# Where weight buffers and streamed operands begin, modulo 256 bytes, in a decoder block on one core

## The chip, the core and the metric

One core of a Trainium2 chip runs the whole block. The metric is the time of one execution in device microseconds; a kernel's time is the median of its runs. All arithmetic on data is float32, and TensorE takes it in the format float32r: each factor is cut into a high part that the format holds exactly and a low part, and a product is made of three (high × high, high × low, low × high).

## The reference

A decoder block with 512 positions and 1024 channels: a mixer of a short gated convolution (A) and sparse attention (B), merged by gates, and a feed-forward part of width 2816 with a short convolution.

```
h = rmsnorm(x, norm1_g);  proj = h @ w_in          # 512 x 1024 by 1024 x 4888
y_a = a_b * causal_dwconv(a_c * a_x, conv_a_w)
y_b = nsa(q, compressed k/v, selected k/v, window k/v, gates)    # 8 heads of 64, 2 groups
mix = gm[:D] * (y_a @ w_a_out) + gm[D:] * (y_b @ w_b_out)
x = x + mix @ w_o
h = rmsnorm(x, norm2_g);  gu = h @ w_ffn_in        # 1024 x 5632
g = causal_dwconv(gu[:, :2816], ffn_conv_w) + ffn_conv_b
x = x + (silu(g) * gu[:, 2816:]) @ w_ffn_out
```

## The kernel before

Activations lie with channels on the partitions and the 512 positions along them. A weight tile of 128 output channels (128 × 1024 float32, 512 KB) comes by one DMA into a raw buffer (`wr`, three of them). ScalarE copies it to the high part (`wh`), and VectorE, GpSimd or a DMA that accumulates on a negated copy makes the low part (`wl`). There are two buffers for each of `wh` and `wl`. `dense` then issues the products: a 128 × 128 block of weights is loaded into TensorE, and 512 columns of the activation's high or low part stream past it (256 in the feed-forward part). Each matmul has a weight load of its own. With `lo_last`, the products of the low weights follow those of the high ones; otherwise they alternate.

The stages, in order of time:

- token projection (`pj`, to 65 us): here the activations `xg_h`, `xg_l` are what is loaded, and the weights stream past them, 348 or 350 columns at a time;
- the convolution's channels (`conv_tile`, `pa`), gates (`gate_tile`, `pg`) and the merge of A (`pma`), with attention's products between them; the streamed operands are `xg_h`, `xg_l` and `ya_h`, `ya_l`;
- the merge of B (`pmb`, past `yb_h`, `yb_l`) and the output projection (`po` from `mix_h`, `mix_l`), eight tiles of 16 + 8 products;
- from 377 us, the feed-forward part: pairs of channel tiles as a two-level product (`ff_pair`) with seven block products of 12 matmuls each. `x_forms` makes seven combinations of the input (`xf_h`, `xf_l`). The weight blocks 11 and 12 come from `wh`, `wl` (or, for some, a low part from the buffers `dl`), the block 22 and the sums of blocks from `th`, `tl`, `sh`, `sl` on the right side of the memory. Quarters of the down projection (`pdn`, past `ah`, `al`) lie between the pairs; the rest follows at the end.

Tile pools are stacks of memory, from the left (`sb`, `pa`, `px`, `pf` and others) and from the right (`pw`, `pb`, `pc` and others). In a pool, tiles follow each other in the order of their first use, each rounded up to 32 bytes. Tiles of one tag share its buffers, and a new tile takes the buffer that comes free first in the scheduler's own simulation, which also orders the instructions of every engine. A raw, `wh` or `wl` buffer is `TOKC` = 1048 words wide, 4192 bytes, or 96 more than a multiple of 256. So two neighbouring buffers begin 96 bytes apart modulo 256.

Where tiles of before begin, modulo 256 (weights left, streamed operands right; the distance is the difference, weight minus streamed):

| weights | begin | streamed | begin |
|---|---|---|---|
| `wh`, first and second buffer | 160, 0 | `xg_h`, `xg_l` | 192 |
| `wl`, first and second buffer | 224, 64 | `ya_h`, `ya_l` | 192, 0 |
| `dl` (low parts made by DMA) | 224 | `yb_h`, `yb_l` | 64, 128 |
| `sh`, `sl`, `th`, `tl` | 224 | `mix_h`, `mix_l`, `ah`, `al` | 224 |
| | | `xf_h`, `xf_l` | 192 |

Blocks within a tile lie 512 bytes apart, and streamed rows 1024 or 2048, so that a tile's place modulo 256 is that of all its blocks.

Of the kernel before, what the change touches and what calls it, by code (L numbers as in the profile page):

```python
# [11 lines left out]
F32 = mybir.dt.float32  # L12
F32R = mybir.dt.float32r
# [5 lines left out]
P = 128  # L19
D = 1024  # L20
S = 512
# [19 lines left out]
C_V = C_Q + 256  # L41
C_G = C_V + 256
TOKC = C_G + 24
NW4 = 5
NWR = 3
NE = 3
# [24 lines left out]
INV_FREQ = (10000.0 ** (-np.arange(HALF) / HALF)).astype(np.float32)  # L71
CH = ((0, 350), (350, 700), (700, TOKC))

# [18 lines left out]
def tile_block(ctx: ExitStack, tc: tile.TileContext, xT, pos, par, par2, w_tok, w_a3, w_gate, w_ao, w_bo, w_o,  # L92
               w_ff, w_dn, c_w1, out):
    nc = tc.nc
    sb = ctx.enter_context(tc.tile_pool(name="sb", bufs=1, side="left"))
    ps = ctx.enter_context(tc.tile_pool(name="ps", bufs=1, space=bass.MemoryType.PSUM))
    in_ctx = ExitStack()
    pa = in_ctx.enter_context(tc.tile_pool(name="pa", bufs=1, side="left"))
# [4 lines left out]

    def const(shape, name, dt=F32, pool=sb):
        return pool.tile(shape, dt, name=name, tag=name)

    def w_tmp(name, shape):

        t = pp.tile([P, TOKC], F32, name=name, tag="w4", bufs=NW4)
        v = t[:, :math.prod(shape)]  # L110
        if len(shape) == 2:
            v = v.rearrange("p (a b) -> p a b", a=shape[0])
        elif len(shape) == 3:
            v = v.rearrange("p (a b c) -> p a b c", a=shape[0], b=shape[1])
        return v
# [4 lines left out]
    def d_bank(name):  # L120
        return bank("d", name, 2)
# [28 lines left out]
    def load_w(src, n, name, first=0, mid=False, pool=False, by_dma=False, lo=None, made=False, mixed=False, after=(), hi=None, cuts=(), pieces=False, then=None):  # L150


        raw = sb.tile([P, TOKC], F32, name=f"wr_{name}", tag="wr", bufs=NWR)
        if hi is None:
            hi = sb.tile([P, TOKC], F32R, name=f"wh_{name}", tag="wh", bufs=2)
        if lo is None:
            lo = sb.tile([P, TOKC], F32R, name=f"wl_{name}", tag="wl", bufs=2)
        if mixed:
            to = raw[:, :n].rearrange("p (k a d) -> p k a d", a=2, d=HD)
            for i in range(2):  # L160
                nc.sync.dma_start(to[:, :, i], src[:, i])
        for a, b in ((0, first), (first, n)) if first else ((0, n),):
            at = [a] + [c for c in cuts if a < c < b] + [b]
            if not mixed:
                for c, d in zip(at, at[1:]) if pieces else ((a, b),):
                    by = nc.scalar if c < 2 * first and not mid else nc.sync
                    loads.append(by.dma_start(raw[:, c:d], src[:, c:d]))
            if then is not None and b == first:
                then()
            for a, b in zip(at, at[1:]):  # L170
                splits.append(nc.scalar.activation(hi[:, a:b], raw[:, a:b], AF.Copy))
                if after:
                    behind(splits[-1], after[0])
                if not made:
                    if by_dma:

                        nc.scalar.activation(lo[:, a:b], raw[:, a:b], AF.Copy, scale=-1.0)
                        nc.gpsimd.dma_start(lo[:, a:b], src[:, a:b], accum_op=ALU.add)
                    else:
                        e = nc.gpsimd if pool else nc.vector  # L180
                        m = e.tensor_sub(lo[:, a:b], raw[:, a:b], hi[:, a:b].bitcast(F32))
                        if after:
                            behind(m, after[1])
                        elif len(x_lows) == 1:
                            behind(m, x_lows[0])
        return hi, lo
# [2 lines left out]
    ones_r = const([P, P], "ones", F32R)  # L189
    ones = ones_r.bitcast(F32)  # L190
    nc.gpsimd.memset(ones, 1.0)
    warm = const([P, 1], "warm")
    wu = d_bank("wu")
    for i in range(NWU):
        nc.tensor.matmul(wu[:, 0:P], ones, ones, start=True, stop=True)
# [12 lines left out]
        return [t_bank(f"pj_t{tt}{i}") for i in range(2)] + [o_bank(f"pj_o{tt}")]  # L208


    def y_tile(name):
        return pa.tile([P, 2, TOKC], F32R, name=name, tag="y", bufs=4)

    tok_lo = [y_tile(f"tok_lo{i}") for i in range(4)]

    def tok_products(tt, bank, k, wh, wl, first, last, sums=False):
        ts_ = slice(tt * P, (tt + 1) * P)
# [102 lines left out]
    def behind(later, earlier):  # L320

        tc.add_manual_dep(later.ins, earlier.ins.name,
                          mybir.DependencyInfo(mybir.DependencyClass.NoSync, mybir.DependencyReason.DATA),
                          reason="order")
# [86 lines left out]
            nc.vector.tensor_tensor(tsin[:, i, :, 0:HALF], ns, ghi, op=ALU.mult)  # L411
            nc.vector.tensor_tensor(tsin[:, i, :, HALF:], sn, glo, op=ALU.mult)

    mhalf = const([P, 12], "mhalf")
    nc.gpsimd.memset(mhalf, -0.5)

    def rsqrt(dst, src, n):
# [40 lines left out]

    def kv_products(i):
        raw = pp.tile([P, 4 * P], F32, name=f"wr_kv{i}", tag="wrkv", bufs=2)  # L460
        hl = sb.tile([P, TOKC], F32R, name=f"wl_kv{i}", tag="wl", bufs=2)
        n = 4 * P
        d = nc.sync.dma_start(raw.rearrange("p (a c) -> p a c", a=2),
                              w_a3[0:2, :, 2 * P * i:2 * P * (i + 1)].rearrange("a p c -> p a c"))
        behind(d, loads[-1])
        loads.append(d)
        nc.scalar.activation(hl[:, 0:n], raw, AF.Copy)
        nc.vector.tensor_sub(hl[:, n:2 * n], raw, hl[:, 0:n].bitcast(F32))

        def products():  # L470
            for kv in range(2):
                if i == 0:
                    kv_acc.append(d_bank(f"pkc{kv}"))
                units = [(hl[:, c:c + P], hl[:, n + c:n + c + P], xg_h[:, 2 * i + k, :], xg_l[:, 2 * i + k, :])
                         for k, c in enumerate((2 * kv * P, (2 * kv + 1) * P))]
                dense(kv_acc[kv], units, first=i == 0, last=i == 3)
        return products

    def between(k):
        if k in kv_made:  # L480
            kv_made.pop(k)()
        if k == KD - 2:
            t = pp.tile([P, TOKC], F32R, name="sq_hl", tag="w4", bufs=NW4)
            sq_hl.extend((t[:, 0:S], t[:, S:2 * S]))
# [32 lines left out]
    r1b, _ = as_rows("n1", r1, scales1[2])  # L517
# [176 lines left out]
                    nc.vector.tensor_sub(kl4[own, :, g, ks], pv[own], kg[own].bitcast(F32))  # L694


    yb_h = y_tile("yb_h").rearrange("p a c -> p (a c)")[:, 0:4 * S].rearrange("p (a s) -> p a s", a=4)
    yb_l = y_tile("yb_l").rearrange("p a c -> p (a c)")[:, 0:4 * S].rearrange("p (a s) -> p a s", a=4)

    ends = {}  # L700

# [113 lines left out]
        nc.gpsimd.tensor_sub(yb_l[dst], yo, yb_h[dst].bitcast(F32))  # L815


    ya_h = y_tile("ya_h").rearrange("p a c -> p (a c)")[:, 0:4 * S].rearrange("p (a s) -> p a s", a=4)
    ya_l = y_tile("ya_l").rearrange("p a c -> p (a c)")[:, 0:4 * S].rearrange("p (a s) -> p a s", a=4)

    def causal_conv(dst, u, w, bias=None):

# [113 lines left out]
        return raw  # L936

    def form_a1(f, n, raw, form):
        h = sb.tile([P, TOKC], F32R, name=f"wh_s{n}_{f}", tag="wh", bufs=2)
        if (f, n) in A1_BY_DMA:  # L940
            l = lo_by_dma(f"s{n}_{f}", raw, w_ff[f, n])
            nc.scalar.activation(h[:, 0:D], raw[:, 0:D], AF.Copy)
        else:
            l = sb.tile([P, TOKC], F32R, name=f"wl_s{n}_{f}", tag="wl", bufs=2)
            ends["a1"] = split(h[:, 0:D], l[:, 0:D], raw[:, 0:D])
        form["a11"] = (h[:, 0:half], l[:, 0:half])
        form["a12"] = (h[:, half:D], l[:, half:D])
# [91 lines left out]
    px = ctx.enter_context(tc.tile_pool(name="px", bufs=1, side="left"))  # L1039
    x1 = const([P, KD, S], "x1", F32, px)  # L1040

    xf_h = const([P, 4, 7, TH], "xf_h", F32R, px)
    xf_l = const([P, 4, 7, TH], "xf_l", F32R, px)
    xv_ctx = ExitStack()
# [39 lines left out]
    _, sums2, r2b, rows2 = row_scales(sq2, "n2", d_bank)  # L1084
# [4 lines left out]
    pf = ctx.enter_context(tc.tile_pool(name="pf", bufs=1, side="left"))  # L1089
    u_bufs = []  # L1090
    for i in range(NU):
        u = const([P, 2, S + 2], f"c{i}", F32, pf)
        nc.gpsimd.memset(u[:, :, 0:2], 0.0)
        u_bufs.append(u)
    a_hl = {}

    def pair_tile(name, tag):
# [72 lines left out]
    def down_weights(f0, n, j0, by_dma=False):  # L1170

        nm = f"d{f0}{j0}"
        per = D // (n * P)
        raw = sb.tile([P, TOKC], F32, name=f"wr_{nm}", tag="wr", bufs=NWR)
        h = sb.tile([P, TOKC], F32R, name=f"wh_{nm}", tag="wh", bufs=2)
        block = lambda t: t[:, 0:D].rearrange("p (j c) -> p j c", j=per)
        src = w_dn[j0:j0 + per, :, f0 * P:(f0 + n) * P].rearrange("j p c -> p j c")
        nc.sync.dma_start(block(raw), src)
        if by_dma:

            l = lo_by_dma(nm, raw, src, block, after={(0, per): ends["sh"], (0, 2 * per): ends["a1"]}.get((f0, j0)))
            m = nc.scalar.activation(h[:, 0:D], raw[:, 0:D], AF.Copy)
            if (f0, j0) == (0, per):
                behind(m, ends["sh"])
        else:
            l = sb.tile([P, TOKC], F32R, name=f"wl_{nm}", tag="wl", bufs=2)
            split(h[:, 0:D], l[:, 0:D], raw[:, 0:D])
        return h, l

# [102 lines left out]
```

## Time and profile before

| what | value |
|---|---|
| median of three runs | 724.03 us (723.95 to 724.71) |
| the profiled execution | 725.49 us, of which the span from first to last instruction is 723.6 |
| TensorE | busy 716.9 us, 4275 matmuls (an fp32 one counts twice) |
| TensorE's weight loads | busy 637.1 us |
| VectorE, ScalarE, GpSimd | 575.6, 415.3, 125.4 us |
| the chain that ended last | 92% TensorE |
| granted clock of TensorE | 1.0 |
| DMA | 88.19 MB, 122 GB/s on average |

How to read it: a row of the timeline or of a group has the line of the kernel, the engine, the operation and the tiles as out<-in, for a matmul out<-streamed,weights. Timeline rows give start and duration in us, and neighbouring instructions of one kind are merged into one row with their count. Group rows give the busy time in us and the mean duration in ns of one instruction. A matmul's duration overlaps with the next matmul's, so the sum of durations is longer than the time.

### The profile page before, as it was taken

The page shows a single profiled execution, that of the slowest core. Times are in us where ns is not written, and L with a number is a line of the kernel's source. Part 1 is how long each engine was busy: PE and PEld are TensorE (multiplying, and loading weights), DVE is VectorE, ACT ScalarE, POOL GpSimd, SP SyncE. Part 2 cuts the span into 40 slices and gives each one's busy share as a digit, 9 for nine tenths or more (in the row PEclk, how much of TensorE's full clock was granted, in tenths as well). Part 3 has the DMA queues.
Part 4 walks back from the last instruction along what each step waited for, and adds up shares of the span by engine and source line. Part 5 has one row for each costly group of instructions (what it writes and reads, how often), then busy time and mean ns, then how long its engine had stood idle before and what let it go on. Part 6 is the DMA issues. An engine that isn't in the chain of part 4 may idle for free.

```text
span 723.6 us, 11196 instructions
## 1 busy us (share of the span) xinstructions
PE 716.9 (99%) x4275; PEld 637.1 (88%) x4275; DVE 575.6 (80%) x988; ACT 415.3 (57%) x706; POOL 125.4 (17%) x111
## 2 busy tenths in 40 slices
PE   8999999999999999999999999999999999999997
PEld 8999788888888888878889999999999999999986
DVE  7978967587666675887876998998898988989833
ACT  7776555777767767544665665565445554455320
POOL 1122443343343201231002011010000010000000
PEclk9999999999999999999999999999999999999999
DMA  8633552211111211336446476545655556552413
GB/s 292 227 89 115 145 119 79 60 68 58 59 59 59 87 60 59 116 124 210 160 131 161 117 175 152 169 119 131 164 143 127 136 127 154 128 146 88 117 30 116
DMA packets 36804, 88.19 MB, mean 122 GB/s; under 512 B 7440, under 2 KB 10896, under 8 KB 36752
## 3 DMA queue, kind: packets, MB, share of 16 engines
q1 hardware_dynamic: 30672, 74.42, 32.3%
q0 software_dynamic: 5648, 12.58, 10.7%
q8 instruction: 33, 0.54, 0.3%
q10 hardware_dynamic: 432, 0.49, 0.2%
q14 instruction: 19, 0.16, 0.1%
HBM read 85.39 MB, written 2.10 MB: 121 GB/s over the span
## 4 chain that ended last, share of the span: by engine, by line
PE 92%; issue 4%; DMA 2%; POOL 0%; ACT 0%; DVE 0%; SPq 0%; POOLq 0%; DVEq 0%
PE p L147 8%; PE p L143 8%; PE p L140 8%; PE pdn L143 4%; PE pdn L140 4%; PE pg L145 4%; PE pg L140 4%; PE pg L143 4%; PE pdn L147 4%; PE pa L140 3%; PE pa L143 3%; PE pt L792 2%; PE po L143 2%; PE po L140 2%; PE po L147 2%
## 5 line engine op out<-in xcount | busy, mean ns | idle before, releaser
L140 PE MATMUL p<-xf_h,sh 128*128 128x256 f32 x352 | 87.3, 281 | 0.0
L143 PE MATMUL p<-xf_l,sh 128*128 128x256 f32 x352 | 87.2, 281 | 0.0
L140 PEld LDWEIGHTS p<-xf_h,sh 128*128 128x128 f32 x352 | 66.3, 188 | 0.0
L143 PEld LDWEIGHTS p<-xf_l,sh 128*128 128x128 f32 x352 | 66.3, 188 | 0.0
L930 DVE TENSOR_TENSOR sl<-s,sh 128x1024 fp32r<-128x1024 f32 x44 | 53.1, 1214 | 3.9 <-ACT sh L929 3.9
L147 PE MATMUL p<-xf_h,sl 128*128 128x256 f32 x352 | 55.8, 281 | 0.0
L929 ACT ACTIVATE sh<-s 128x1024 fp32r<-128x1024 f32 x44 | 45.6, 1051 | 17.4 <-DVE s L974 13.2
L955 POOL DMA_DIRECT2D wl_d<-in_w_dn_dram x16 | 19.1, 1195 | 207.2 <-ACT wl_d L952 207.2
L143 PE MATMUL pdn<-al,wh_d 128*128 128x512 f32 x134 | 52.6, 393 | 0.0
L140 PE MATMUL pdn<-ah,wh_d 128*128 128x512 f32 x134 | 52.2, 392 | 0.0
L140 PE MATMUL pg<-xg_h,wh_g 128*128 128x512 f32 x128 | 51.0, 399 | 0.0
L145 PE MATMUL pg<-xg_h,wl_g 128*128 128x512 f32 x128 | 50.8, 397 | 0.0
L143 PE MATMUL pg<-xg_l,wh_g 128*128 128x512 f32 x128 | 50.5, 395 | 0.0
L147 PEld LDWEIGHTS p<-xf_h,sl 128*128 128x128 f32 x352 | 47.9, 188 | 0.3
L743 ACT ACTIVATE e<-sc,mx 128x512 f32<-128x512 f32 (+3 forms) x64 | 33.3, 525 | 18.8 <-DVE mx L742 16.4
L140 PE MATMUL p<-xf_h,wh_s 128*128 128x256 f32 x176 | 43.5, 280 | 0.0
L143 PE MATMUL p<-xf_l,wh_s 128*128 128x256 f32 x176 | 43.4, 281 | 0.0
L140 PE MATMUL pa<-xg_h,wh_a 128*128 128x512 f32 x96 | 38.2, 398 | 0.0
L143 PE MATMUL pa<-xg_l,wh_a 128*128 128x512 f32 x96 | 37.9, 395 | 0.0
L796 DVE TENSOR_TENSOR pl<-pt,ph 128x512 fp32r<-128x512 f32 x40 | 27.3, 685 | 10.8 <-ACT ph L795 10.4
L769 ACT ACTIVATE e<-e,sums 128x512 f32<-128x512 f32 (+3 forms) x64 | 30.9, 556 | 7.5 <-DVE sums L719 7.5
L929 ACT ACTIVATE th<-wr_s 128x512 fp32r<-128x512 f32 x20 | 12.6, 630 | 38.7 <-issue 28.3
(361 smaller groups left out, 2133.5 us busy)
## 6 DMA issues: line engine op xcount, KB each, us to landing
wr_s<-in_w_ff_dram SPq DMA_DIRECT2D x44, 512.0 KB, 3.6
wr_d<-in_w_dn_dram SPq DMA_DIRECT2D x22, 512.0 KB, 3.7
wr_g<-in_w_gate_dram SPq DMA_DIRECT2D x16, 512.0 KB, 3.5
wl_d<-in_w_dn_dram POOLq DMA_DIRECT2D x16, 512.0 KB, 7.0
wr_a<-in_w_a_dram SPq DMA_DIRECT2D x12, 512.0 KB, 3.5
wr_t<-in_w_tok_dram SPq DMA_DIRECT2D x10, 524.0 KB, 5.8
wr_o<-in_w_o_dram SPq DMA_DIRECT2D x8, 512.0 KB, 3.7
wr_ao<-in_w_ao_dram SPq DMA_DIRECT2D x4, 512.0 KB, 3.5
```

What stands on the lines that cost most here:

```text
L140: m = nc.tensor.matmul(acc, wh, xh, start=first and i == 0, stop=False)
L143: nc.tensor.matmul(acc, wh, xl, start=False, stop=False)
L145: m = nc.tensor.matmul(acc, wl, xh, start=False, stop=last and i == n - 1)
L147: m = nc.tensor.matmul(acc, wl, xh, start=False, stop=last and i == n - 1)
L743: nc.scalar.activation(e[:, i, 0:nk], sc[:, o:o + nk], AF.Exp, bias=mx[:, i], accum_out=sums[:, i])
L769: nc.scalar.activation(v, v, AF.Copy, scale=sums[:, i])
L792: ends["pt"] = nc.tensor.transpose(pt[:, i * P:(i + 1) * P], e[:, i, kt * P:(kt + 1) * P], ident)
L796: m = nc.vector.tensor_sub(pl, pt, ph.bitcast(F32))
L929: m = nc.scalar.activation(h, v, AF.Copy)
L930: nc.vector.tensor_sub(l, v, h.bitcast(F32))
L955: nc.gpsimd.dma_start(view(l), src, accum_op=ALU.add)
```

## The change

The buffers of `wh` and `wl` leave the pool `sb` for a pool `ws` of their own at the left end, each with a name of its own (`wh0`, `wh1`, `wl0`, `wl1`), and `w_tile` gives them out in turn. A tile of 1024 words begins 96 bytes into the first buffer of a kind and at the start of the second; the second `wl` buffer is 64 bytes longer. The constants `warm` and `mhalf` become two parts of one tile. The four tiles `y` get names of their own too, and `ya`, `yb` begin 64 bytes times their number into them. A pad of 32 bytes stands ahead of `xf_h` and one of 192 bytes ahead of the feed-forward part's tiles `cv`, `up`, `ah`, `al`, `dl`.

By the order and sizes of the tiles this puts all of `wh`, `wl`, `dl`, `xg`, `ya`, `yb`, `ah`, `al` at 224 modulo 256, where `mix`, `sh`, `sl`, `th` and `tl` stay, and `xf_h`, `xf_l` at 0. The distance is then 0 for the products of 512 columns in `dense`, and 224 (that is, −32) for those of 256 columns in `ff_pair`. Raw buffers move from 192, 32, 128 to 96, 192, 32.

```diff
+LINE = 256
+XF_PAD = 8
+PF_PAD = 48
...
+    ws = ctx.enter_context(tc.tile_pool(name="ws", bufs=1, side="left"))
     sb = ctx.enter_context(tc.tile_pool(name="sb", bufs=1, side="left"))
...
+    w_count = {"wh": 0, "wl": 0}
+
+    def w_tile(kind, name, n=D):
+        slot = w_count[kind] % 2
+        w_count[kind] += 1
+        width = TOKC + (2 * LINE // 32 if kind == "wl" and slot else 0)
+        t = ws.tile([P, width], F32R, name=f"{kind}_{name}", tag=f"{kind}{slot}")
+        return t[:, 0:n] if n > D or slot else t[:, TOKC - D:TOKC - D + n]
...
         if hi is None:
-            hi = sb.tile([P, TOKC], F32R, name=f"wh_{name}", tag="wh", bufs=2)
+            hi = w_tile("wh", name, n)
         if lo is None:
-            lo = sb.tile([P, TOKC], F32R, name=f"wl_{name}", tag="wl", bufs=2)
+            lo = w_tile("wl", name, n)
...
-    warm = const([P, 1], "warm")
+    half_warm = const([P, 13], "half_warm")
+    mhalf, warm = half_warm[:, 0:12], half_warm[:, 12:13]
...
-    def y_tile(name):
-        return pa.tile([P, 2, TOKC], F32R, name=name, tag="y", bufs=4)
-
-    tok_lo = [y_tile(f"tok_lo{i}") for i in range(4)]
+    def y_tile(name, i):
+        return pa.tile([P, 2, TOKC], F32R, name=name, tag=f"y{i}")
+
+    def y_mix(name, i):
+        o = i * LINE // 16
+        return y_tile(name, i).rearrange("p a c -> p (a c)")[:, o:o + 4 * S].rearrange("p (a s) -> p a s", a=4)
+
+    tok_lo = [y_tile(f"tok_lo{i}", i) for i in range(4)]
...
-    mhalf = const([P, 12], "mhalf")
...
-        hl = sb.tile([P, TOKC], F32R, name=f"wl_kv{i}", tag="wl", bufs=2)
+        hl = w_tile("wl", f"kv{i}")
...
-    yb_h = y_tile("yb_h").rearrange("p a c -> p (a c)")[:, 0:4 * S].rearrange("p (a s) -> p a s", a=4)
-    yb_l = y_tile("yb_l").rearrange("p a c -> p (a c)")[:, 0:4 * S].rearrange("p (a s) -> p a s", a=4)
+    yb_h = y_mix("yb_h", 2)
+    yb_l = y_mix("yb_l", 3)
...
-    ya_h = y_tile("ya_h").rearrange("p a c -> p (a c)")[:, 0:4 * S].rearrange("p (a s) -> p a s", a=4)
-    ya_l = y_tile("ya_l").rearrange("p a c -> p (a c)")[:, 0:4 * S].rearrange("p (a s) -> p a s", a=4)
+    ya_h = y_mix("ya_h", 0)
+    ya_l = y_mix("ya_l", 1)
...
+    const([P, XF_PAD], "xf_pad", F32, px)
     xf_h = const([P, 4, 7, TH], "xf_h", F32R, px)
...
+    const([P, PF_PAD], "pf_pad", F32, pf)
     a_hl = {}
```

The same replacement by `w_tile` stands in `form_a1` and `down_weights`.

More of the change, by code (lines that the diff above doesn't have):

```diff
@@ L938, in form_a1 @@
     def form_a1(f, n, raw, form):
-        h = sb.tile([P, TOKC], F32R, name=f"wh_s{n}_{f}", tag="wh", bufs=2)
+        h = w_tile("wh", f"s{n}_{f}")
         if (f, n) in A1_BY_DMA:
@@ L943, in form_a1 @@
         else:
-            l = sb.tile([P, TOKC], F32R, name=f"wl_s{n}_{f}", tag="wl", bufs=2)
+            l = w_tile("wl", f"s{n}_{f}")
             ends["a1"] = split(h[:, 0:D], l[:, 0:D], raw[:, 0:D])
@@ L1174, in down_weights @@
         raw = sb.tile([P, TOKC], F32, name=f"wr_{nm}", tag="wr", bufs=NWR)
-        h = sb.tile([P, TOKC], F32R, name=f"wh_{nm}", tag="wh", bufs=2)
+        h = w_tile("wh", nm)
         block = lambda t: t[:, 0:D].rearrange("p (j c) -> p j c", j=per)
@@ L1185, in down_weights @@
         else:
-            l = sb.tile([P, TOKC], F32R, name=f"wl_{nm}", tag="wl", bufs=2)
+            l = w_tile("wl", nm)
             split(h[:, 0:D], l[:, 0:D], raw[:, 0:D])
```

## The prediction

> **What bounds the kernel now.** I read the page first, then TensorE's waits, then its timeline. The time belongs to TensorE. Its busy time fills 99% of the span, its instructions are 92% of the chain that ended last, and the one wait it has in the last two thirds of the run is 1.0 us long (the view of waits, TensorE's own).
>
> ```profile
> span 723.6 us, 11196 instructions
> ...
> PE 716.9 (99%) x4275; PEld 637.1 (88%) x4275; DVE 575.6 (80%) x988; ACT 415.3 (57%) x706; POOL 125.4 (17%) x111
> ...
> PE 92%; issue 4%; DMA 2%; POOL 0%; ACT 0%; DVE 0%; SPq 0%; POOLq 0%; DVEq 0%
> ...
> PE p L147 <- DMA wl_s<-in_w_ff_dram: 1.0, 1, 1.0
> ```
>
> So what counts is how far apart the matmuls start. I call that the stride; a matmul's listed duration also holds a tail that the next one overlaps, so strides are read from starts in the timeline. Every matmul here has its own weight load, which starts with the matmul before it: weights of the next and columns of the running one are read at the same time. I call (weight start − start of the streamed operand) modulo 256 bytes the distance. The change sets nothing else of size, so the question is whether strides depend on it. The addresses are those the allocator gave the kernel before.
>
> The output projection is a natural experiment. Its eight last products (mix_h past wl_o) use two weight buffers in turn: with the first at distance 0, with the second at 96.
>
> ```profile
> 339.61 2.02 PE L147 MATMUL po<-mix_h,wl_o 128*128 128x512 f32 x8
> 341.70 2.03 PE L147 MATMUL po<-mix_h,wl_o 128*128 128x512 f32 x8
> 347.24 1.98 PE L147 MATMUL po<-mix_h,wl_o 128*128 128x512 f32 x8
> 352.79 2.04 PE L147 MATMUL po<-mix_h,wl_o 128*128 128x512 f32 x8
> 358.33 1.98 PE L147 MATMUL po<-mix_h,wl_o 128*128 128x512 f32 x8
> 360.15 0.39 PE L140 MATMUL po<-mix_h,wh_o 128*128 128x512 f32 x1
> 363.88 2.03 PE L147 MATMUL po<-mix_h,wl_o 128*128 128x512 f32 x8
> 369.54 1.98 PE L147 MATMUL po<-mix_h,wl_o 128*128 128x512 f32 x8
> ```
>
> A row of eight holds seven strides and one duration of 0.39. Distance 96: (2.03 − 0.39)/7 = 0.234, in all three. Distance 0: 0.227 in three tiles, but 0.233 in the first (2.02). From 358.33 to 360.15 are eight strides, 0.2275. So the distance does matter, by some 3%, and distance 0 knows two beats: a quick one, 0.2271, and a slow one, about 0.2325. Which of them a run falls into seems to hang on how it was entered.
>
> **The change part by part.** *512-column products outside attention.* All go to distance 0: 816 for gates, convolution, its merge and the compressed keys, 288 for the attention merge and the output projection, 510 for the down projection. What they have now:
>
> ```profile
> 300.22 0.39 PE L140 MATMUL pg<-xg_h,wh_g 128*128 128x512 f32 x1
> ...
> 304.15 0.39 PE L145 MATMUL pg<-xg_h,wl_g 128*128 128x512 f32 x1
> ```
> ```profile
> 88.52 0.39 PE L140 MATMUL pa<-xg_h,wh_a 128*128 128x512 f32 x1
> ...
> 89.92 0.39 PE L140 MATMUL pa<-xg_h,wh_a 128*128 128x512 f32 x1
> ```
> ```profile
> 506.31 0.39 PE L140 MATMUL pdn<-ah,wh_d 128*128 128x512 f32 x1
> ...
> 508.15 1.09 PE L147 MATMUL pdn<-ah,wl_d 128*128 128x512 f32 x4
> ...
> 554.53 1.07 PE L147 MATMUL pdn<-ah,wl_d 128*128 128x512 f32 x4
> ```
>
> First buffers (distances 224 and 32): 17 strides in 3.93, 0.2312. Second buffers (64): 6 strides in 1.40, 0.2333. Mean 0.2322 for the 816. The down projection has 192 in its first eight products, 1.84/8 = 0.2300, and already 0 in its last four: three strides and a duration in 1.09, 0.2333, or in 1.07, 0.2267; the two beats again, the slow one in the greater part of such rows. With 0.2323 for these, the 510 stand at 0.2308. The 288 I put at 0.2308 too: the output projection's group below has a mean duration of 394 ns against the down projection's 393.
>
> After the change I take 0.2298, the middle of the two beats: the long rows above favour the quick one, the short ones the slow one. Gain: 816 × 2.4 ns = 2.0 us, 288 × 1.0 = 0.3, 510 × 1.0 = 0.5; together 2.8. Bounds: all quick (0.2271), 816 × 5.1 + 798 × 3.7 = 7.1 us of gain; all slow (0.2325), 816 × 0.3 + 798 × 1.7 = 1.6 us of loss.
>
> *Feed-forward products, 256 columns.* 22 pairs of channel tiles with 84 products each, 1848. Now distance 32 for the sums and the 22 block (sh, sl, th, tl), and 224, 64 or 128 for the 11 and 12 blocks, by buffer; afterwards 224 throughout, since the input lies 32 bytes beyond the weights.
>
> ```profile
> 503.83 0.28 PE L143 MATMUL p<-xf_l,sh 128*128 128x256 f32 x1
> ...
> 506.31 0.39 PE L140 MATMUL pdn<-ah,wh_d 128*128 128x512 f32 x1
> ```
> ```profile
> 398.03 0.28 PE L140 MATMUL p<-xf_h,wh_s 128*128 128x256 f32 x1
> ...
> 398.96 0.28 PE L147 MATMUL p<-xf_h,wl_s 128*128 128x256 f32 x1
> ...
> 426.82 0.28 PE L140 MATMUL p<-xf_h,wh_s 128*128 128x256 f32 x1
> ...
> 428.36 0.28 PE L140 MATMUL p<-xf_h,sh 128*128 128x256 f32 x1
> ...
> 677.78 0.28 PE L140 MATMUL p<-xf_h,wh_s 128*128 128x256 f32 x1
> ...
> 678.74 0.40 PE L147 MATMUL p<-xf_h,wl_s 128*128 128x256 f32 x2
> ```
>
> Distance 32: 21 strides in 2.48, 0.1181. Distance 224, which the first wh buffer has today: 8 in 0.93 (0.1163), 13 in 1.54 (0.1185), 8 in 0.96 (0.1200). All 29: 3.43/29 = 0.1183; the first kind comes in more tiles than the last, so I weigh it double, 4.36/37 = 0.1178. Gain 1848 × 0.3 ns = 0.6 us. Bounds: always 0.1163, 3.3 us gained; always 0.1200, 3.5 us lost.
>
> The costliest groups by line give the counts (352 = 22 pairs × 4 blocks × 4) and the durations:
>
> ```profile
> L140 PE MATMUL p<-xf_h,sh 128*128 128x256 f32 x352 | 87.3, 281 | 0.0
> ...
> L143 PE MATMUL pdn<-al,wh_d 128*128 128x512 f32 x134 | 52.6, 393 | 0.0
> ...
> L140 PE MATMUL po<-mix_h,wh_o 128*128 128x512 f32 x64 | 25.1, 394 | 0.0
> ```
>
> *Token projection and attention.* In the projection weights and streamed operand change roles and columns start every 1400 bytes, so distances are spread before and after: 0, bounded by the spread between buffers above, 288 × ±3 ns = ±0.9 us. The attention tiles lie on the right side and keep their addresses: 0.
>
> *Weight buffers with names of their own.* They now alternate strictly. Before they did too, except once: wh_d of down quarter 1 took the buffer left by the first product's weights, and the next wh_s waited 2.71 us for quarter 0's. These two swap.
>
> ```profile
> 434.63 1.05 ACT L1182 ACTIVATE wh_d<-wr_d 128x1024 fp32r<-128x1024 f32 x1
> 441.49 1.06 ACT L929 ACTIVATE wh_s<-wr_s 128x1024 fp32r<-128x1024 f32 x1 [2.71 <-PE pdn L143]
> ...
> 444.58 0.39 PE L140 MATMUL pdn<-ah,wh_d 128*128 128x512 f32 x1
> ```
> ```profile
> 435.70 0.38 SPq L1178 DMA_DIRECT2D wr_d<-in_w_dn_dram  x1
> ```
>
> wh_d would then be made at 441.5 to 442.6, 2.0 us ahead of its first use at 444.58, so 0. Queued behind it: the raw buffer it reads is held 7 us longer, so SP's load of the following wr_d leaves at 442.6 rather than 435.7, lands by about 446.3 (3.7 us in the page's DMA part), and ACT's negated copy of it, with th and sh behind it, slips 2 us. If that cover fails: at most 2 us, once. POOL's accumulating load starts behind that copy; its tile is used 15 us later.
>
> *The merged constant and pads.* No instruction is added. ACT writes warm and POOL reads mhalf in one tile now; ACT writes at 34.5, long before POOL's first reading at 39.1: 0. VectorE's offsets change too, but 16 subtractions over two buffers took 1206 to 1226 ns: 0.
>
> ```profile
> L402 ACT ACTIVATE warm<-n_t x1: 203/203/203, 34.5 to 34.5; 128x1 f32<-128x1 f32 x1
> L419 POOL TENSOR_TENSOR r_n<-ms_n,mhalf x2: 1048/1258/1467, 39.1 to 384.5; 128x4 f32<-128x4 f32 x2
> L930 DVE TENSOR_TENSOR wl_s<-wr_s,wh_s x16: 1206/1217/1226, 444.5 to 669.0; 128x1024 fp32r<-128x1024 f32 x16
> ```
>
> What is late next is VectorE, by the table of stages (TensorE, weight loads, VectorE, ScalarE, GpSimd; then the granted clock, 1.00):
>
> ```profile
> 450.00:650.00 200.00, 200.00 (x1396) 186.71 (x1395) 180.78 (x239) 102.50 (x124) 15.50 (x13) 1.00 0.56 143
> ```
>
> It is busy 180.8 of these 200 us; TensorE's gain there is under 1%, so it keeps slack and takes nothing back.
>
> Sum: 2.8 + 0.6 = 3.4 us. The profiled execution took 725.49 (span 723.6 and 1.9 around it), 1.46 above the median of the runs; 722.1 by it, and by the median 724.03 − 3.4 = 720.6.
>
> **The rivals.** *It does nothing (724.0).* The strides could be set by something that moved with the buffers. For it: the 256-column groups hardly differ (0.1181 and 0.1178). Against it: 2.03 and 1.98 in turn, with nothing else changed.
> The Trainium skill (TensorE: Matmul & The Clock Gate, section "Step-by-step: what each phase is for") speaks against the change: two independent read ports, so that "Loading the next tile's weights doesn't steal SBUF read bandwidth from the running matmul". By that rule no distance matters and the time stays at 724.0; the alternating rows do not agree.
>
> *Quick beats everywhere.* With one distance throughout, a quick run is never broken up: 7.1 + 3.3 = 10.4, giving 713.6. For it: three rows of 1.98, whose strides stay even over eight products. Against it: the 1.09 rows.
>
> *Slow beats everywhere (slower).* One regular layout also holds a bad beat fast, where today changing distances shake it out: 1.6 + 3.5 = 5.1, giving 729.1. For it: 677.78, eight equal slow strides. With the 512-column products at 0.2325 it decides from a feed-forward stride of 0.1180 up.
>
> **How the numbers follow.** Chances: mixed beats 0.50 (720.6, own range 718 to 722.5), quick 0.22 (713.6 up to 718), nothing 0.15, slow 0.13. Differences under 0.2%, 1.45 us, can't be told from none here. Mixed and quick are faster, 0.72; nothing is the same, 0.15; slow is slower, 0.13. Range: 713.6 to 725.5, which leaves out the slow case and little of the quick.
>
> **What the profile will show.** Right: rows of eight wl_o products at 1.98 in both buffers, gate and convolution strides below 0.230, feed-forward strides below 0.118. Wrong: rows at 2.02 or above in the out projection, feed-forward strides at 0.120, or new waits of PE on ACT around 440 us. The prediction falls if entry states, which I can't read from the trace, pick one beat for most runs.

## The result, and the profile after

The changed kernel takes 716.22 us (median of five runs, 715.61 to 717.05), the kernel before on the same chip 723.98 (723.76 to 724.71): a ratio of 0.9892, 95% interval 0.9878 to 0.9907. The gain is 7.8 us where 3.4 were forecast. The profiled execution took 716.42 us, span 714.5. That of before took 725.49, 1.5 above its median, so the two traces differ by 9.1 us. That is 1.3 more than the medians do.

The head of the page after the change, its chain, and TensorE's only wait in the feed-forward part:

```profile
span 714.5 us, 11190 instructions
...
PE 709.0 (99%) x4275; PEld 635.7 (89%) x4275; DVE 574.1 (80%) x988; ACT 415.5 (58%) x706; POOL 127.3 (18%) x111
...
PE 92%; issue 4%; DMA 2%; DVE 1%; POOL 0%; ACT 0%; POOLq 0%; SPq 0%; DVEq 0%
```
```profile
PE p L161 <- DMA wl_s<-in_w_ff_dram: 0.6, 1, 0.6
```

Every engine has as many busy instructions as before (the six that are missing are semaphore instructions), and the chain and the bound are the same. TensorE's busy time fell by 7.9 us, that of no other engine moved by more than 2. So the strides, read as before from starts, should carry the difference. The output projection first (TensorE's timeline; start, duration, count at the end):

```profile
335.72 1.98 PE L161 MATMUL po<-mix_h,wl_o 128*128 128x512 f32 x8
337.76 1.98 PE L161 MATMUL po<-mix_h,wl_o 128*128 128x512 f32 x8
343.20 1.98 PE L161 MATMUL po<-mix_h,wl_o 128*128 128x512 f32 x8
...
365.10 1.98 PE L161 MATMUL po<-mix_h,wl_o 128*128 128x512 f32 x8
```

The alternation of 1.98 and 2.03 is gone: every row is quick, whichever buffer it reads. Next come 20 products of a gate tile, two neighbouring down-projection groups of 12 (8 with the high weights, 4 with the low ones), and 48 feed-forward products:

```profile
296.06 0.39 PE L154 MATMUL pg<-xg_h,wh_g 128*128 128x512 f32 x1
...
300.59 0.39 PE L159 MATMUL pg<-xg_h,wl_g 128*128 128x512 f32 x1
```
```profile
499.90 0.39 PE L154 MATMUL pdn<-ah,wh_d 128*128 128x512 f32 x1
...
502.65 0.39 PE L154 MATMUL pdn<-ah,wh_d 128*128 128x512 f32 x1
...
505.37 0.28 PE L154 MATMUL p<-xf_h,wh_s 128*128 128x256 f32 x1
...
508.17 0.28 PE L154 MATMUL p<-xf_h,sh 128*128 128x256 f32 x1
...
510.97 0.28 PE L154 MATMUL p<-xf_h,sh 128*128 128x256 f32 x1
```

Gates: 20 strides in 4.53, 0.2265. Down projection: 12 in 2.75, 0.2292, and the next 12 in 2.72, 0.2267. Feed-forward: 24 in 2.80, 0.1167, and once more. The table sums the times from start to start over all products of a kind, and its last column has their mean in ns, without those that hold a wait or a change to another kind of work:

| products | before, us | after, us | saved | forecast | mean stride |
|---|---|---|---|---|---|
| gates, convolution, its merge, compressed keys (816) | 191.9 | 189.1 | 2.8 | 2.0 | 232.0 → 228.9 |
| attention's merge, output projection (288) | 66.7 | 65.3 | 1.4 | 0.3 | 231.5 → 226.7 |
| down projection (510) | 117.6 | 116.2 | 1.4 | 0.5 | 230.6 → 227.8 |
| feed-forward (1848) | 219.8 | 216.7 | 3.1 | 0.6 | 118.2 → 116.7 |

Together these are 8.7 of the 9.1 us between the traces. Some 0.4 of the feed-forward part's 3.1 are shorter stalls, the DMA wait of 1.0 and now 0.6 among them. By the strides alone (count times the difference of the means) the terms are 2.5, 1.4, 1.4 and 2.7, together 8.0, which is close to the 7.8 of the medians. Every term is too small in the forecast, and the feed-forward one by a factor of 4 to 5.

### The profile page after: what moved, and what is told of

Same layout as the page of the kernel before. It is cut to its first block, busy times and chain, and to the rows that moved or that the text cites. A ratio compares the mean times of both kernels' runs of the same rounds, so it can differ in the third digit from the quotient of the medians.

```text
span 714.5 us, 11190 instructions
## 1 busy us (share of the span) xinstructions
PE 709.0 (99%) x4275; PEld 635.7 (89%) x4275; DVE 574.1 (80%) x988; ACT 415.5 (58%) x706; POOL 127.3 (18%) x111
## 4 chain that ended last, share of the span: by engine, by line
PE 92%; issue 4%; DMA 2%; DVE 1%; POOL 0%; ACT 0%; POOLq 0%; SPq 0%; DVEq 0%
PE p L154 8%; PE p L161 8%; PE p L157 8%; PE pdn L157 4%; PE pdn L154 4%; PE pg L159 4%; PE pg L157 4%; PE pg L154 4%; PE pdn L161 4%; PE pa L154 3%; PE pa L157 3%; PE pt L810 2%; PE po L161 2%; PE po L157 2%; PE po L154 2%
## 5 line engine op out<-in xcount | busy, mean ns | idle before, releaser
L161 PE MATMUL pdn<-ah,wl_d 128*128 128x512 f32 x128 | 34.2, 389 | 0.0
```

Source lines behind the costliest of these rows:

```text
L161: m = nc.tensor.matmul(acc, wl, xh, start=False, stop=last and i == n - 1)
```

## Experiments

My theory after this: the distance sets the stride by itself, and what counts is the value into which a long run settles; the "slow beat" at distance 0 was only the run-in of runs that ended too soon. (A run is a series of products of one kind without others between them; its run-in is the uneven part at its start, before the strides repeat.) Rivals: the order that came with the new names; an evenness of the layout, whatever its distance; other traffic that moved with the buffers.

**Each distance by itself.** The block is replaced by runs of 64 matmuls from two tiles, `W` (weights) and `X` (streamed), without DMA or other engines beside them. The index `k` stands for a distance of 32 × k bytes; in the third round `X` is moved instead of `W`.

```diff
+    for n, count in ((512, 64), (256, 64)):
+        for ks, by_x in ((up, False), (up[::-1], False), ([0, 3, 6, 1, 4, 7, 2, 5], True)):
+            for k in ks:
...
```

> The block is left out: the kernel only runs long unbroken runs of 64 matmuls with a weight load each, at the eight distances (weight start minus streamed start, modulo 256 bytes) 0, 32, ... 224, tile Da to Dh, three times in different order, first 512 columns, then 256; nothing else runs beside them. In the third round the streamed operand is moved instead of the weights. Theory 1 (each distance has a stride of its own, reached within about ten products from any entry): 512 columns settle at 226.7 ns for distance 0 in all three rounds; 233 for 32, 233.5 for 64, 234 for 96, 232 for 128, 229.5 for 192, 233 for 224. 256 columns settle at 116.7 for 224, 118.3 for 32, 117.5 for 64. Theory 2 (any distance that stays the same settles on the quick beat; the change gained by evenness): 226.7 and 116.7 at every distance. Theory 3 (the beat depends on the absolute place of weights or on traffic of other engines): the third round differs from the first two, or all strides agree here.

Its timeline; `Da` is distance 0, `Db` 32, `Dc` 64, `Dd` 96, and so on to `Dh`, 224:

```profile
239.40 29.18 PE L126 MATMUL Da_x<-X,W 128*128 128x512 f32 x128
268.42 15.15 PE L126 MATMUL Dd_x<-X,W 128*128 128x512 f32 x64
283.41 14.82 PE L126 MATMUL Dg_x<-X,W 128*128 128x512 f32 x64
298.07 15.08 PE L126 MATMUL Db_x<-X,W 128*128 128x512 f32 x64
...
387.94 7.70 PE L126 MATMUL Dc_x<-X,W 128*128 128x256 f32 x64
...
425.78 15.10 PE L126 MATMUL Dh_x<-X,W 128*128 128x256 f32 x128
...
471.03 7.42 PE L126 MATMUL Dc_x<-X,W 128*128 128x256 f32 x64
478.29 7.73 PE L126 MATMUL Db_x<-X,W 128*128 128x256 f32 x64
485.86 15.52 PE L126 MATMUL Da_x<-X,W 128*128 128x256 f32 x128
```

Settled strides in ns, from the starts after the first 24 of each run:

| distance | 0 | 32 | 64 | 96 | 128 | 160 | 192 | 224 |
|---|---|---|---|---|---|---|---|---|
| 512 columns | 226.7 | 233.3 | 233.4 | 234.3 | 232.5 | 233.3 | 228.9 | 233.3 |
| 256 columns | 120.0 | 118.4 | 117.8 or 113.3 | 117.4 | 118.6 | 120.0 | 117.8 | 116.7 |

With nothing beside it, distance 0 saves 5.8 to 7.6 ns in 512 columns against all others but 192 (2.2), and shares the worst place in 256. So other traffic isn't needed for the difference. Which of the two tiles moves makes none (128 at 512 columns alone shifted, to 233.2). At 64 a 256-column run has two lasting values: 7.70 and 7.42 are the same 64 products. The Trainium skill (TensorE: Matmul & The Clock Gate, section "Step-by-step: what each phase is for") lets weights and moving data be read without disturbing each other; these rows, 226.7 to 234.3 by distance alone, do not agree.

**Names alone.** The kernel before with strict alternation of its weight buffers, the buffers' places as they were.

```diff
-            hi = sb.tile([P, TOKC], F32R, name=f"wh_{name}", tag="wh", bufs=2)
+            hi = w_tile("wh", f"{name}")
...
```

Here `w_tile` gives out the tags `wh0` and `wh1` in turn, in the pool `sb`.

> The kernel before with strictly alternating weight buffers and nothing else; because of the one swap the two wh buffers change roles in the feed-forward part (some 190 products of 256 columns go from distance 64 to 224, some 200 of 512 columns in the down projection from 192 to 32). Theory 1: 724.0 + 200 x 3.2 ns - 190 x 0.5 ns = 724.5. Rival (the gain comes from the order of instructions that the strict alternation gives): 716 to 720.

724.72 us, ratio 1.0009 (1.0000 to 1.0019). The order that strict alternation gives is not the cause.

**Two partial undoings.** In the changed kernel, first the feed-forward input moved to distance 32, then `xg`, `ya` and `yb` by 192 bytes, which puts 912 products of 512 columns at 64.

```diff
-XF_PAD = 8
-PF_PAD = 48
+XF_PAD = 56
+PF_PAD = 0
```
```diff
+    const([P, 48], "pa_pad", F32, pa)
     xg_h = const([P, KD, S], "xg_h", F32R, pa)
...
```

> The changed kernel with the feed-forward input moved so that its 1848 products have distance 32 instead of 224, everything else in place. Theory 1: 1848 x (118.3 - 116.7) = 3.0 us more, 719.2. Theory 2 (evenness is enough): 716.2.

> The changed kernel with xg, ya, yb 192 bytes further on, so that the 912 products of gates, convolution, merges and compressed keys have distance 64 instead of 0; the token projection's distances move too. Theory 1: 912 x (233.6 - 228.4) = 4.7 us more, 720.9. Theory 2: 716.2.

718.83 us (ratio 0.9930, 0.9918 to 0.9943) and 720.78 (0.9950, 0.9938 to 0.9963): 2.6 and 4.6 us of the gain are lost, where the expectations, from strides, say 3.0 and 4.7. Both layouts still have one distance for all products of a kind, so evenness is not the cause.

**Feed-forward at distance 0.** Only the pad ahead of `xf_h` is left out.

> The changed kernel with the 32 bytes ahead of the feed-forward input left out, so that its distance is 0 as it is for the 512-column products. Theory (settled strides: 120.0 ns at 0, 116.7 at 224): 716.2 + 1846 x 3.3 ns = 722.4, so that about four fifths of the gain of the change is lost again. Rival (what counts is only that every distance is the same throughout): 716.2. Rival (0 is best for every width): below 716.2.

721.87 us, ratio 0.9973 (0.9964 to 0.9983); the products' mean stride is 119.9. So 5.7 us of 7.8 are given back by one offset of 32 bytes, and "the same place for all" is wrong advice at 256 columns.

**Run length at distance 0.** The block is left out again; runs of 4, 8, 16 and 32 at distance 0 (`Da`) stand between runs of 8 at 96 (`Dd`).

> The block is left out; only matmuls from two tiles in a fixed order, without other traffic. First part, 512 columns: runs of 4, 8, 16 and 32 at distance 0 between runs of 8 at distance 96. Theory (at distance 0 a run starts in an uneven beat of about 232 ns and falls into an even one of 226.7 after at most 10 products, which it keeps): the mean stride at distance 0 falls with the length, from up to 232 in runs of 4 to about 227 to 228 in runs of 32; distance 96 stays at 233 to 235 whatever stands between. Rival (distance 0 has two lasting beats, and the entry picks one): runs of 4 and of 32 have the same two values, each kept for the whole run. Second part: 4, 8, 16, 240 and 248 bytes; both operands moved by 32 or 96 together, and 256 bytes apart (theory: all three as distance 0, 226.7; if the absolute place counted, otherwise); 32 with 96 (weights 128, streamed 384: distance 0 modulo 256 minus 256, as 0). Third part, 256 columns at distance 64 behind each other distance: which entries find 113.3 and which 117.8.

```profile
28.71 1.09 PE L143 MATMUL Da_x<-X,W 128*128 128x512 f32 x4
29.63 2.03 PE L143 MATMUL Dd_x<-X,W 128*128 128x512 f32 x8
...
34.29 2.01 PE L143 MATMUL Da_x<-X,W 128*128 128x512 f32 x8
36.15 2.02 PE L143 MATMUL Dd_x<-X,W 128*128 128x512 f32 x8
...
62.11 3.81 PE L143 MATMUL Da_x<-X,W 128*128 128x512 f32 x16
65.76 2.03 PE L143 MATMUL Dd_x<-X,W 128*128 128x512 f32 x8
...
89.71 7.44 PE L143 MATMUL Da_x<-X,W 128*128 128x512 f32 x32
96.99 2.03 PE L143 MATMUL Dd_x<-X,W 128*128 128x512 f32 x8
```

From start to start: 4 products 0.230, 8 at 0.2325, 16 at 0.2281, 32 at 0.2275. The single strides of the last run are 236, 229, 232, 231, then 227, 226, 227 to its end. In all 12 runs of 16 and 32 the uneven part lasts four products, once eight, and never comes back. The 1.09 row of four is the same as the 1.09 rows of the down projection before the change, and 0.2325 is the "slow beat" of the prediction to the digit: a run-in, not a beat. The distance counts modulo 256: both tiles moved by 32 or by 96, and 256 bytes either way, settle at 226.6 to 226.7. It is finer than 32 bytes, though: 4, 8, 16, 240 and 248 bytes give 232.3, 230.3, 233.1, 228.7 and 233.3 (from the starts after the first 24 of 32). The same run has 256 columns at finer distances: 48, 56, 60, 68, 72 and 80 bytes give 117.7 to 119.3, none of them the 113.3 that 64 can have, and 216 gives 120.0, though 224 has 116.7.

**Down projection at 192.** The changed kernel without the 192-byte pad: groups of 8 products at 192 and 4 at 0, as before the change.

> The changed kernel without the pad ahead of the feed-forward part's tiles: the first eight products of each down-projection group stand at distance 192 as they did before the change, the last four at 0. All feed-forward products but 32 stay at 224. By the settled strides alone (228.9 ns at 192 against 226.7): 384 x 2.2 ns = 0.8 us more than the changed kernel's 716.2, that is 717.0. Theory that the beat of a short run hangs on what ran just before it: 512-column groups of 8 + 4 never settle, as before (230.6 against 227.8: 510 x 2.8 ns = 1.4 us), and the feed-forward runs behind them may fall into one of the slower beats at 224 (118 ns: 1846 x 1.3 = 2.4 us more, 120 ns: 6 us), so 717.6 with the feed-forward part at 116.7, 720 at 118, 724 at 120. The rival that only each product's own distance counts gives 717.0.

716.86 us, ratio 0.9907 (0.9893 to 0.9920); by the starts the down projection takes 117.1 us instead of 116.2, the feed-forward part stays in its quick value at 224 (116.9). The time alone can't be told from the changed kernel's. The mean stride of the 510, 229.6, lies above the 228.3 that 382 at 228.9 and 128 at 226.7 would give: the run-in again. A poorer entry from the down projection did not spoil the feed-forward runs at 224.

**Feed-forward at 64, where two values last.**

```diff
+XF_PAD = 48
+PF_PAD = 8
```

> The changed kernel with the feed-forward input moved so that the distance of all 1846 feed-forward products is 64 instead of 224; everything else stays. Theory (the stride is the value into which a long run at that distance settles; in the sweep 64 settled at 117.8 ns in one entry and at 113.3 in two): in runs of 84 products the floor of 113.3 is found early and kept, against 116.7 at distance 224, so 1846 x 3.3 ns = 6.1 us less than the changed kernel's 716.2, that is 710.1; if most runs enter the other value, 716.2 + 1846 x 1.1 ns = 718.2. The rival that strides in the kernel are set by other traffic and evenness of layout gives 716.2 in both cases.

717.14 us, ratio 0.9911 (0.9894 to 0.9927): neither. The timeline shows both values, one early, one late:

```profile
385.94 0.28 PE L154 MATMUL p<-xf_h,sh 128*128 128x256 f32 x1
...
387.30 0.28 PE L154 MATMUL p<-xf_h,sh 128*128 128x256 f32 x1
```
```profile
506.74 0.28 PE L154 MATMUL p<-xf_h,sh 128*128 128x256 f32 x1
...
508.15 0.28 PE L154 MATMUL p<-xf_h,sh 128*128 128x256 f32 x1
```

12 strides in 1.36, 0.1133, and 12 in 1.41, 0.1175. From 384 us one run of 303 products keeps 113.3 to its end. From 436 us on, each run behind a down-projection group has 117.8, and none leaves it. So here the entry does decide, and for as long as the run lasts.

**What picks the value.** The block left out; 24 to 26 products of 512 columns at 0, then some of 256 columns at another distance, then 36 at 64 (`Dc`).

> The block is left out; matmuls from two tiles in a fixed order, without other traffic: 24, 25 or 26 products of 512 columns at distance 0, then 0 to 24 of 256 columns at another distance, then 36 at distance 64. Theory (the beat that a run at 64 keeps is picked by the phase in which it starts, and so by what ran last): directly behind 512 columns 117.8; behind 12 or 24 products at 224 or 192 113.3; behind one or two of them not yet. Rival (chance of each entry): the same sequence gives both values in its three repeats.

```profile
21.88 4.40 PE L127 MATMUL Dc_x<-X,W 128*128 128x256 f32 x36
...
88.28 0.39 PE L127 MATMUL Dh_x<-X,W 128*128 128x256 f32 x2
88.51 4.24 PE L127 MATMUL Dc_x<-X,W 128*128 128x256 f32 x36
...
98.06 0.29 PE L127 MATMUL Dh_x<-X,W 128*128 128x256 f32 x1
98.19 4.41 PE L127 MATMUL Dc_x<-X,W 128*128 128x256 f32 x36
```

Behind 512 columns 117.8 (4.40); behind two products at 224 already 113.3 (4.24); behind one, 117.8. I had expected that two would not yet do. 12 at 224, 192, 160, 128 or 32 hand over to 113.3, that is, the run at 64 behind them has that value; 12 at 0 or 96 do not. All three repeats of each sequence agree: it is the sequence, not chance.

The distance of what stands before does not decide by itself, though. In the run on lengths, whose third part let 24 products at another distance lead to 48 at 64, those at 224 and 192 handed over to 113.3, but those at 128 (`De`), 160 and 32 left the run at 117.8, where 12 of them hand over here:

```profile
251.22 3.01 PE L143 MATMUL De_x<-X,W 128*128 128x256 f32 x24
254.06 5.82 PE L143 MATMUL Dc_x<-X,W 128*128 128x256 f32 x48
...
276.52 2.96 PE L143 MATMUL Dh_x<-X,W 128*128 128x256 f32 x24
279.32 5.60 PE L143 MATMUL Dc_x<-X,W 128*128 128x256 f32 x48
```

In the sweep, 64 products at 96 led to 113.3, where 12 and 24 do not. So the number of products ahead, or what stands before them, counts too. Without the block, 224 (from two products on) and 192 (12 and 24) handed over each time. A rule that covers all of these entries is not shown.

**Handing over in the kernel.** Two pads on the right side put the products of `sh`, `sl`, `th`, `tl` at 64 (1320 of 1848 by the groups of the profile; the expectations count 1313 of 1846), those of `wh`, `wl`, `dl` stay at 224. A second kernel, with other pads, has 192 in place of 224. The first one's edit:

```diff
+    pz = ctx.enter_context(tc.tile_pool(name="pz", bufs=1, side="right"))
+    const([P, 40], "pz_pad", F32, pz)
     pw = ctx.enter_context(tc.tile_pool(name="pw", bufs=1, side="right"))
...
+    pz2 = mx_ctx.enter_context(tc.tile_pool(name="pz2", bufs=1, side="right"))
+    const([P, 24], "pz2_pad", F32, pz2)
     pc = mx_ctx.enter_context(tc.tile_pool(name="pc", bufs=1, side="right"))
```

> The changed kernel with two pads among the tiles on the right, so that the feed-forward products whose weights are sums or the 22 block (sh, sl, th, tl: 1313 of 1846) stand at distance 64, and those from wh, wl, dl stay at 224. Each pair of channel tiles begins with 24 products at 224. Theory (at 64 two beats last, 113.3 and 117.8 ns; behind products at 224 the run without other traffic went over to 113.3, behind 512-column products at 0 to 117.8): the 1313 settle at 113.3 instead of 116.7, 4.4 us less than the changed kernel's 716.2, that is 711.8. If the entry from 224 does not carry over into the kernel: 1313 at 117.8, 716.2 + 1.4 = 717.6. Rival that the kernel's stride is set by the mean over distances or by an even layout: 716.2 or more.

> As the run before, but the products from wh, wl, dl at 192 instead of 224 (the input 64 bytes beyond the weights, sh, sl, th, tl 64 behind it). Theory: 533 at 117.8 (0.6 us more), 1313 at 113.3 (4.4 less), so 712.4 if 192 hands over to the quick beat at 64, as it did in its one entry without other traffic; 718.2 if not, since the beat at 192 has the same sequence (117, 119, 117, 118, 118) as the slower one at 64.

The first: 713.18 us (712.88 to 714.46), ratio 0.9853 (0.9838 to 0.9867), below the changed kernel's 0.9892 with intervals that do not touch. It is the best of these kernels. Its timeline where the kernel with 64 throughout had 0.1175:

```profile
506.67 0.28 PE L154 MATMUL p<-xf_h,sh 128*128 128x256 f32 x1
...
508.05 0.28 PE L154 MATMUL p<-xf_h,sh 128*128 128x256 f32 x1
...
510.76 0.28 PE L154 MATMUL p<-xf_h,sh 128*128 128x256 f32 x1
```
```profile
L154 PE MATMUL p<-xf_h,sh 128*128 128x256 f32 x352 | 84.8, 277 | 0.0
```

12 strides in 1.38 (0.1150, the run-in), then 24 in 2.71, 0.1129 within the rounding of 0.1133. Of the 1320, 84% have at most 114 ns; the rest are run-ins and some stretches up to 460 us, the longest from 411 to 427. The forecast of 711.8 came out 1.4 low for that reason and because the down projection's mean is 229.0 instead of 227.8 in this trace. Against the trace of the changed kernel, strides in the feed-forward part save 3.4 us; another 0.8 is its DMA wait, which did not occur here.

The second: 715.19 us, ratio 0.9882 (0.9864 to 0.9900), six runs from 713.23 to 718.04. Its profiled execution lies at the low end and shows the handover in most runs (89% at 114 or less). The longer executions have no trace. Their spans are on record: 712.8 to 714.4 us against 711.3 for the profiled one, and 714.3 for the execution of 718.04. A handover that failed everywhere (718.2, less the 1.9 us around the span) would need 716.3, so it can have failed in part at most, and what made them longer stays open.

## Why the prediction was partly right, and where it failed

The direction, the bound and the reading of the natural experiment held (one row of it, 2.04, gives 0.236 and not 0.234, which changes nothing). Eight out-projection products at 1.98 in either buffer, gate and convolution strides below 0.230 (228.9 and 228.4 ns) and feed-forward strides below 0.118 are all there. The strides taken for the kernel before held as well: 232.2, 230.8, 230.8 and 118.1 ns against 232.0, 231.5, 230.6 and 118.2 over the whole trace. What failed are the strides taken for the kernel after, and with them the size of the gain.

- *Names, constants, order: 0.* Right: names alone give 1.0009 (the merged constant and the pads were not tried alone). The waits around 440 us stayed on ScalarE, as the cover named there required (ScalarE's timeline after the change: `wh_d` behind the down projection, nothing of TensorE behind it):

```profile
436.76 1.07 ACT L1202 ACTIVATE wh_d<-wr_d 128x1024 fp32r<-128x1024 f32 x1 [2.88 <-PE pdn L157]
```

- *512 columns: 2.8 us.* The step that failed is "distance 0 knows two beats", and the middle between them, 0.2298. There is one lasting value, 0.2267, and a run-in to it, mostly of 4 to 10 products. Before the change no run at distance 0 was longer than 8, so the run-ins stood in the trace as rows of their own. The measured 5.5 us (2.8, 1.4 and 1.4, rounded; 5.3 by strides alone) lie closer to the bound that I called all quick, 7.1, than to 2.8. What is missing to it is where runs are still cut: attention's products between gate and convolution tiles (228.9), down-projection groups entered from 256 columns (227.8). The uncut output projection has 226.7.
- *Feed-forward: 0.6 us.* The step that failed is the weighing of three sequences at distance 224 (0.1163, 0.1185, 0.1200) by the number of tiles. In the kernel before, these products stood singly or in runs of at most 13, behind other distances. In the changed kernel they stand in long runs, and all of these but one settle at a mean of 116.7, by the sequence 117, 117, 116 or 113, 116, 118, 120; long runs with the kernel left out do the same. So the term is 2.7 us by strides, and not 0.6. The exception is a run of 39 products from 378.88 us, between two groups of small products of the norm (`pr_n`): it keeps 117.7 (119, 116, 118 and the like). With the kernel left out a sequence 119, 116, 118 at 224 came too, behind runs at 232 and 240. So 224 has a second value as well, and what ran before seems to pick it. Flat 120 at 224 appeared in the old kernel alone (alone, 216 has it); what set it is open.
- *The rivals.* "It does nothing" falls with the sweep. "Slow beats everywhere" (729.1) falls: none lasts at 512 columns and distance 0. "Quick beats everywhere", 713.6 up to 718 and given 0.22, is the case that came, and by its own reason: a quick run is no longer broken up. "Entry states pick one beat", named as what would make the forecast fall, shows in the changed kernel in that one run of 39 only; it rules at 256 columns and distance 64, not where I feared it.

What in the memory or in TensorE makes the distance count was not tried. Only float32r products of 256 and 512 columns were, with blocks 512 bytes apart and a weight load for each.

## What to carry to other kernels

When the bound is TensorE and each matmul brings a weight load, measure the stride for each distance between weights and streamed operand modulo 256, per width, in long runs by themselves: here it was worth up to 3% at 512 columns and 6% at 256, and the best distance differs by width. A value read from runs of 4 to 13 products is a run-in until a longer run has shown that it lasts; take the settled one for a layout that will make the runs long. Where two values last, look at what runs just before, since two products at another distance, or their number, decided which.

## What was not expected of the hardware

Two steady strides for the same instructions: 113.3 and 117.8 ns at 256 columns and distance 64, each kept for as long as nothing interrupts (303 and 168 products in a row), and picked by what ran ahead: in the short sequences two products at 224 were enough. And the distance counts below 32 bytes: 4 bytes off costs 5.6 ns of 226.7.
